# Hybrid RWKV-7 / retention / attention block: a block-diagonal state chain, matmuls issued in groups by tile shape, modulation weights in pairs of blocks

## The chip, the cores and the metric

The kernel runs on one core of a Trainium2 chip. The metric is the device time of one execution in microseconds (us); the kernel before was run three times. A separate execution was profiled, and every row below comes from it.

## The reference

Two layers of one trunk over 512 tokens (256 context tokens, then 256 latent ones) of width 1024. Per layer: a modulated RMSNorm; one input projection; three token mixers side by side (RWKV-7 in both directions, retention, multi-head latent attention); a gated merge; then a modulated RMSNorm and a SwiGLU, dense in layer 0 and top-2 of 8 experts in layer 1. The modulation comes from `c @ w_mod + b_mod`. What matters here is the RWKV-7 mixer, 8 heads of 64 channels, both directions:

```python
def step(S, xs):
    r_t, w_t, k_t, v_t, kk_t, a_t = xs
    sa = jnp.einsum('bhij,bhj->bhi', S, -kk_t)
    S = (S * w_t[:, :, None, :] + sa[..., None] * (kk_t * a_t)[:, :, None, :]
         + v_t[..., None] * k_t[:, :, None, :])
    return S, jnp.einsum('bhij,bhj->bhi', S, r_t)
```

## The kernel before

All data is 32 bit. The projections run with operands split into a high and a low part in the one-pass 32-bit type (`mm3`, L917 to L919, three matmuls); an ordinary 32-bit matmul is issued as two passes, so counts of such matmuls in the trace are twice those of the code.

The RWKV-7 scan is done in chunks of 64 tokens. A *unit* is a pair of heads (`p`, four of them) in one direction (`d`), so a layer has 8 units of 8 chunks. For each unit:

- `rwkv_elem` makes decays and keys; `lora_up` is part of it: a product with the high half `hi` of the weights (L260, 128 rows) and one with the low half `lo` (L261, the 64 rows of the direction).
- `rwkv_prod` makes the products of keys within the chunks (L389, on 64 rows, two halves of the chunks), masks them into `MX`, and calls `rwkv_inverse`, which inverts the unit triangular matrices: much VectorE work, then four groups of 32 x 32 matmuls (L564, L573, L592, L602) into the transposed inverse `TF`, one 64-column block per chunk and head.
- `rwkv_trans` transposes keys and values; the values go to rows 64 to 127 of `UV`.
- `rwkv_chain` goes through the chunks in order. A chunk: L625 (with the state `S`) and L627 (`MX` with `UV`) add up in PSUM; VectorE copies them to `Pb` (L630); L636 multiplies by `TF` per head; ScalarE copies the result into rows 0 to 63 of `UV` (L638); L641 gives the state's update; VectorE adds it (L646). After each four chunks the outputs are made (L658, L662, on 64 columns).

`weave` draws these generators together: while unit u's chain is emitted, products and transposes of u+1, the elements of u+2 and *fill* are emitted between, each in proportion to a written number of steps. Fill is projection work whose results are spilled to DRAM (`spill`) and, in units 0 to 3, the modulation (`mods`). `NFILL` and `MODF` say how many steps of each go into a unit. What fill is left goes under attention and retention (`attend`).

`mods` takes 128-row blocks of `w_mod`; four matmuls of 32 columns each (L1031) per block. It yields after each block; `modnorm`, `ffn`, `run` and `fill` draw these yields. Raw weights of the projections and of the modulation share a ring of four buffers (`wraw`), loaded on SyncE's queue.

The order on each engine isn't that of the program text: a planner places instructions by a rank, which is the place in program order, among those whose operands it reckons to be ready. `tc.high_priority(n)` lowers the rank of what is emitted inside by n.

Of the kernel before, what the change touches and what calls it, by code (L numbers as in the profile page):

```python
# [24 lines left out]
def build_consts():  # L25
# [15 lines left out]

    strict = strict & (p[:, None] >= 64)
# [89 lines left out]
class Kern:  # L132
# [14 lines left out]

    def cst(s, name):
        o, w = CB[name]
        return s.consts[:, o:o + w]  # L150
# [91 lines left out]
    def lora_weights(s, i):  # L242
# [3 lines left out]
        lo = s.tile(s.rp, [128, 512], f"wlo{i}", F32R)  # L246
        for d in range(2):
            own = HRS[d]
            raw = s.tile(s.rp, [128, 512], ("rF", "kF", "vF", "kk")[i * 2 + d])
            for hr in HRS:  # L250
                nc.sync.dma_start(raw[hr], s.I["lw2"][s.l, own, i * 512:i * 512 + 512])
            nc.gpsimd.tensor_copy(hi[:, d], raw)
            nc.gpsimd.tensor_tensor(lo[own], raw[own], hi[own, d].bitcast(F32), ALU.subtract)
        return hi, lo

    def lora_up(s, ps, i, d, p):

        (hi, lo), X = s.lw[i], s.lx[i]
        rows, cols = HRS[d], slice(p * 128, p * 128 + 128)
        s.nc.tensor.matmul(ps, hi[:, d, cols], X[:, d], start=True, stop=False)  # L260
        s.nc.tensor.matmul(ps, lo[rows, cols], X[rows, d], start=False, stop=True)  # L261
# [111 lines left out]
    def rwkv_prod(s, U):  # L373
# [4 lines left out]
        MX = s.mxs[s.nmx % 2]  # L378
        s.nmx += 1
        mk = s.cst(f"mask{U.d}")  # L380
        for half in range(2):
# [4 lines left out]
            for cc in range(4):  # L386
                c = half * 4 + cc
                for h, hr in enumerate(HRS):
                    nc.tensor.matmul(px[h][:, cc * 128:cc * 128 + N], U.BK[hr, c].rearrange("p a b -> p (a b)"), U.LA[hr, c].rearrange("p a b -> p (a b)")[:, 0:N], start=True, stop=True)  # L389
# [12 lines left out]
    def rwkv_trans(s, U):  # L402

        nc, rp = s.nc, s.rp
        ident = s.cst("ident")
        U.BT = BT = s.tile(rp, [128, 8, 128], "BT")
# [13 lines left out]
        for odd in range(2):  # L420
            nc.scalar.copy(UV[64:128].rearrange("p (c o) v -> p c o v", o=2)[:, :, odd], pv[odd * 64:odd * 64 + 64].rearrange("p (c v) -> p c v", v=128))

# [27 lines left out]
    def rwkv_run(s, proj):  # L450

        s.tts = [s.tile(s.rp, [128, 17 * 64], f"TT{j}") for j in range(2)]
        s.las = [s.tile(s.rp, [128, 8, 2, 64], f"LA{j}") for j in range(3)]
        s.mxs = [s.tile(s.rp, [128, 8, 2, 128], f"MX{j}") for j in range(2)]
# [3 lines left out]
        s.ntt = s.nuv = s.nsd = s.nla = s.nmx = 0  # L458
        for t in s.tts + s.sds:
            s.nc.gpsimd.memset(t, 0.0)  # L460
        for t in s.uvs:
            s.nc.gpsimd.memset(t[0:64], 0.0)

        if s.t0:
            for t in s.las:
                s.nc.gpsimd.memset(t[:, 0:s.t0 // 64, 1], 0.0)
            for t in s.mxs:
                s.nc.gpsimd.memset(t[:, 0:s.t0 // 64, :, 64:128], 0.0)
# [14 lines left out]
        for u in range(-1, 8):  # L483
# [21 lines left out]
    def rwkv_inverse(s, Ac, FT):  # L505
# [64 lines left out]
        for u in range(8):  # L570
            for qd in range(4):
                qr = slice(qd * 32, qd * 32 + 32)
                nc.tensor.matmul(pe[qr, u * 32:u * 32 + 32], ET[qr, u, :], Q[qr, u, :], start=True, stop=True)  # L573
# [9 lines left out]
        TT = TF[:, 0:1024].rearrange("p (c h t) -> p c h t", c=8, h=2)  # L583
        for h in range(2):
            a, b = slice(h * 64, h * 64 + 32), slice(h * 64 + 32, h * 64 + 64)
            nc.scalar.mul(TT[0:32, :, h, 0:32], E2T[a], -1.0)
            nc.scalar.mul(TT[32:64, :, h, 32:64], E2T[b], -1.0)
        p2 = s.tile(s.ps, [128, 512], "iv")
        for u in range(8):
            for h in range(2):  # L590
                a, b = slice(h * 64, h * 64 + 32), slice(h * 64 + 32, h * 64 + 64)
                nc.tensor.matmul(p2[b, u * 32:u * 32 + 32], FT[a, u, :], E2[a, u, :], start=True, stop=True)  # L592
# [6 lines left out]
        for u in range(8):  # L599
            for h in range(2):  # L600
                a, b = slice(h * 64, h * 64 + 32), slice(h * 64 + 32, h * 64 + 64)
                nc.tensor.matmul(pg[a, u * 32:u * 32 + 32], Q2[b, u, :], E2T[b, u, :], start=True, stop=True)  # L602
        yield
        for h in range(2):
            a = slice(h * 64, h * 64 + 32)
            nc.scalar.copy(TT[0:32, :, h, 32:64], pg[a, 0:256].rearrange("p (u c) -> p u c", c=32))
        return TF

    def rwkv_chain(s, U):
# [12 lines left out]
        for k, c in enumerate(order):  # L622
            ch = s.tile(s.ps, [128, 512], "ch")
            if k:
                mm(ch[:, 0:128], LA[:, c].rearrange("p a b -> p (a b)"), S[:, k - 1], start=True, stop=False)  # L625
            for h in range(2):
# [8 lines left out]
            for h in range(2):  # L635
                mm(ch[:, 128 + h * 64:192 + h * 64], U.TF[:, (2 * c + h) * 64:(2 * c + h) * 64 + 128], Pb[:, hs[h]], start=True, stop=True)  # L636
# [13 lines left out]
            if c >= c0o and k % 4 == 3:  # L650
# [3 lines left out]
                for j in (g * 4, g * 4 + 2):  # L654
                    cb = j % 4 * 64
                    for odd, hr in enumerate(HRS):
                        if j + odd != order[0]:
                            mm(po[hr, cb:cb + 128], LA[:, j + odd, 1, :], S[:, order.index(j + odd) - 1], start=True, stop=False)  # L658
                    for h in range(2):
                        for odd, hr in enumerate(HRS):  # L660
                            first = j + odd == order[0]
# [1282 lines left out]
```

## Time and profile before

| what | value |
|---|---|
| three runs | 2420.04, 2423.49, 2425.33 us (median 2423.49) |
| the profiled execution's own time | 2412.98 us |
| its span, first to last instruction | 2411.2 us |
| TensorE matmul busy | 2262.6 us (94%) |
| VectorE busy | 1538.5 us (64%) |
| ScalarE busy | 1170.4 us (49%) |
| GpSimd busy | 355.6 us (15%) |
| DMA, mean over the span | 155 GB/s |
| mean granted TensorE clock | 0.97 |

The profiled execution took 1.8 us more than its span, and 10.5 us less than the median of the three runs. Matmuls are pipelined: in a timeline the distance from one start to the next says what one costs, not its duration.

### The profile page before, as it was taken

Reading aid. Unit: us, or ns where it says so; the run is one execution under the profiler, and the core shown is the slowest. Engines: PE = TensorE matmul, PEld = TensorE weight load, DVE = VectorE, ACT = ScalarE, POOL = GpSimd, SP = SyncE. Lnnn points to the kernel's source line nnn. Section 1 sums busy time; section 2 is a strip of 40 time slices with the busy share of each in tenths; the row PEclk is TensorE's granted clock in tenths of the full one; section 3 lists DMA queues with packets and bytes.
Section 4 is the critical chain, followed back from the end, with each engine's and each line's share of the span. In section 5 each row is a group of like instructions: output and inputs, shape, how many; then the busy total and the mean of one; then the engine's idle time right before and its main releaser. Section 6 shows DMA issues by size and latency. Waiting matters only on the chain. (4 is left out here: it accounts for less than half of the span.)

```text
span 2411.2 us, 41643 instructions
## 1 busy us (share of the span) xinstructions
PE 2262.6 (94%) x15772; PEld 1785.6 (74%) x15772; DVE 1538.5 (64%) x2994; ACT 1170.4 (49%) x2150; POOL 355.6 (15%) x307
## 2 busy tenths in 40 slices
PE   7989999999999989999998999999998989999996
PEld 4767777787667767778876777878867768878775
DVE  5776666655566453333227678777567578888897
ACT  4544444544543342222226554565363457777765
POOL 1311112101002210000013221130111211111120
PEclk9999999999999999999999999999899989999998
DMA  7343432223235424443223333322325658988895
GB/s 259 110 141 127 139 122 71 76 87 117 94 113 157 160 81 162 169 162 104 95 79 124 111 113 117 115 65 91 114 71 162 216 174 320 336 306 318 309 319 192
DMA packets 160609, 373.69 MB, mean 155 GB/s; under 512 B 18016, under 2 KB 35424, under 8 KB 160400
## 3 DMA queue, kind: packets, MB, share of 16 engines
q1 hardware_dynamic: 160400, 370.94, 45.9%
q8 instruction: 126, 2.06, 0.4%
q14 instruction: 83, 0.68, 0.1%
HBM read 345.18 MB, written 25.69 MB: 154 GB/s over the span
## 5 line engine op out<-in xcount | busy, mean ns | idle before, releaser
L895 DVE TENSOR_TENSOR wlo<-wraw,whi 128x512 fp32r<-128x512 f32 (+4 forms) x666 | 652.6, 1001 | 347.9 <-ACT whi L893 334.7
L893 ACT CAST whi<-wraw 128x512 fp32r<-128x512 f32 (+4 forms) x666 | 536.8, 820 | 557.2 <-PE mm L918 226.6
L917 PE MATMUL fl<-xh,whi 128*128 128x512 f32 (+1 forms) x816 | 317.0, 389 | 2.8 <-ACT whi L893 2.7
L919 PE MATMUL fl<-xh,wlo 128*128 128x512 f32 (+1 forms) x816 | 306.7, 376 | 6.7 <-DVE wlo L895 6.5
L918 PE MATMUL fl<-xl,whi 128*128 128x512 f32 (+1 forms) x816 | 302.4, 371 | 0.0
L919 PEld LDWEIGHTS fl<-xh,wlo 128*128 128x128 f32 x816 | 157.7, 193 | 31.6 <-DVE wlo L895 10.0
L917 PEld LDWEIGHTS fl<-xh,whi 128*128 128x128 f32 x816 | 158.0, 194 | 27.9 <-issue 6.0
L918 PEld LDWEIGHTS fl<-xl,whi 128*128 128x128 f32 x816 | 158.2, 194 | 21.3 <-issue 4.7
L917 PE MATMUL mm<-xh,whi 128*128 128x512 f32 (+1 forms) x416 | 165.6, 400 | 2.0 <-ACT pad L1797 1.0
L919 PE MATMUL mm<-xh,wlo 128*128 128x512 f32 (+1 forms) x416 | 162.5, 391 | 3.2 <-DVE wlo L895 3.1
L918 PE MATMUL mm<-xl,whi 128*128 128x512 f32 (+1 forms) x416 | 163.5, 393 | 0.0
L918 PE MATMUL mm<-wlo,xgh 128*128 128x512 f32 (+1 forms) x384 | 146.5, 381 | 15.3 <-DVE wlo L895 14.8
L917 PE MATMUL mm<-whi,xgh 128*128 128x512 f32 (+1 forms) x384 | 144.3, 378 | 0.2 <-ACT xs L1665 0.2
L919 PE MATMUL mm<-whi,xgl 128*128 128x512 f32 (+1 forms) x384 | 143.7, 374 | 0.0
L1696 POOL TENSOR_TENSOR H<-H,yt 128x512 f32<-128x512 f32 x29 | 56.1, 1960 | 392.5 <-DVE yt L1695 392.5
L918 PEld LDWEIGHTS mm<-wlo,xgh 128*128 128x128 f32 x384 | 72.2, 188 | 37.0 <-DVE wlo L895 27.0
L917 PEld LDWEIGHTS mm<-xh,whi 128*128 128x128 f32 x416 | 78.3, 189 | 27.3 <-ACT whi L893 4.9
L919 PEld LDWEIGHTS mm<-xh,wlo 128*128 128x128 f32 x416 | 78.4, 188 | 20.9 <-DVE wlo L895 4.9
L636 PEld LDWEIGHTS ch<-Pb,TT 128*128 128x128 f32 x512 | 71.8, 194 | 26.2 <-DVE Pb L630 17.3
L918 PEld LDWEIGHTS mm<-xl,whi 128*128 128x128 f32 x416 | 78.6, 189 | 16.3 <-DVE xl L711 0.8
L646 DVE SCALAR_TENSOR_TENSOR Sd<-ch,e2c,Se 64x64 f32<-64x64 f32 x192 | 53.8, 280 | 56.0 <-PE ch L641 53.4
L636 PE MATMUL ch<-Pb,TT 128*128 128x64 f32 x512 | 79.3, 278 | 8.9 <-DVE Pb L630 8.1
(527 smaller groups left out, 4688.1 us busy)
## 6 DMA issues: line engine op xcount, KB each, us to landing
wraw<-in_ws_dram SPq DMA_DIRECT2D x284, 512.0 KB
wraw<-in_ws_dram SPq DMA_DIRECT2D x302, 256.0 KB
wraw<-in_w_mod_dram SPq DMA_DIRECT2D x96, 256.0 KB
wraw<-in_ws_dram SPq DMA_DIRECT2D x64, 384.0 KB
wraw<-in_w_mod_dram SPq DMA_DIRECT2D x32, 512.0 KB
wm<-in_w_mod_dram SPq DMA_DIRECT2D x32, 256.0 KB
spg<-stg SPq DMA_DIRECT2D x24, 256.0 KB
mth<-spg SPq DMA_DIRECT2D x24, 256.0 KB
```

Source lines behind the costliest of these rows:

```text
L636: mm(ch[:, 128 + h * 64:192 + h * 64], U.TF[:, (2 * c + h) * 64:(2 * c + h) * 64 + 128], Pb[:, hs[h]], start=True, stop=True)
L646: nc.vector.scalar_tensor_tensor(S[hr, k, hr], ch[hr, o], e2c[hr, c, :], Se[hr, hr], ALU.mult, ALU.add)
L893: s.nc.scalar.copy(hi, raw)
L895: s.follow(s.nc.vector.tensor_sub(lo, raw, hi.bitcast(F32)))
L917: mm(out, ah, bh, start=start, stop=False)
L918: mm(out, ah, bl, start=False, stop=False)
L919: mm(out, al, bh, start=False, stop=stop)
L1696: eng.tensor_tensor(s.h[2 + i][:, ns], s.h[2 + i][:, ns], t, ALU.add)
```

## The change

- The chain's product of `MX` with the values is made before the chain, for all eight chunks of a unit at once, in `rwkv_trans`: 16 matmuls on quarter-array tiles (64 rows by 64 columns) into one PSUM tile, copied by ScalarE into rows 0 to 63 of `UV` (the refill). The chain later overwrites those rows as before.
- In a chunk, VectorE adds that part to L625's product, once per head, into the two diagonal blocks of a zeroed `Pd`; for the first chunk it copies. `TF` now holds the two heads' blocks below one another, and one matmul of 128 columns takes the place of the two of 64.
- `lo` of the lora weights has 128 rows with zeros in the other direction's half, so that L261 runs on all 128 rows.
- Groups of matmuls of one tile shape (`rwkv_prod`, the new product, four in `rwkv_inverse`, the outputs, a pair of modulation blocks) are emitted under `together()`, which is `high_priority(60)`.
- `mods` takes two blocks per yield; the step counts that draw it are halved.
- `rwkv_trans` is woven with 28 steps instead of 4; in layer 1, `NFILL` for units is 12 instead of 9.
- `MX` comes from the pool instead of two fixed tiles, and some memsets go.

```diff
+    def together(s):
+        return s.tc.high_priority(60)
...
     def lora_weights
-        lo = s.tile(s.rp, [128, 512], f"wlo{i}", F32R)
+        lo = s.tile(s.rp, [128, 2, 512], f"wlo{i}", F32R)
+        nc.gpsimd.memset(lo.bitcast(F32), 0.0)
...
-            nc.gpsimd.tensor_tensor(lo[own], raw[own], hi[own, d].bitcast(F32), ALU.subtract)
+            nc.gpsimd.tensor_tensor(lo[own, d], raw[own], hi[own, d].bitcast(F32), ALU.subtract)
...
     def lora_up
-        s.nc.tensor.matmul(ps, lo[rows, cols], X[rows, d], start=False, stop=True)
+        s.nc.tensor.matmul(ps, lo[:, d, cols], X[:, d], start=False, stop=True)
...
     def rwkv_trans
+        while U.MX is None:
+            yield
+        pm = s.tile(s.ps, [128, 512], "aa")
+        with s.together():
+            for c in range(8):
+                for h, hr in enumerate(HRS):
+                    nc.tensor.matmul(pm[hr, c * 64:c * 64 + 64], U.MX[64:128, c, h, 0:64], UV[64:128, c, hr], start=True, stop=True)
+        yield
+        for hr in HRS:
+            nc.scalar.copy(UV[0:64, :, hr], pm[hr].rearrange("p (c v) -> p c v", v=64))
...
     def rwkv_run
-        s.tts = [s.tile(s.rp, [128, 17 * 64], f"TT{j}") for j in range(2)]
+        s.tts = [s.tile(s.rp, [128, 9 * 64], f"TT{j}") for j in range(2)]
+        s.pds = [s.tile(s.rp, [128, 128], f"Pd{j}") for j in range(2)]
...
-                st.append((f"trans{u + 1}", s.rwkv_trans(U[u + 1]), 4))
+                st.append((f"trans{u + 1}", s.rwkv_trans(U[u + 1]), 28))
...
     def rwkv_inverse (and so for the other three groups)
-        for u in range(8):
-            for qd in range(4):
-                qr = slice(qd * 32, qd * 32 + 32)
-                nc.tensor.matmul(pq[qr, u * 32:u * 32 + 32], F16[qr, u, :], E[qr, u, :], start=True, stop=True)
+        with s.together():
+            for u in range(8):
+                for qd in range(4):
+                    qr = slice(qd * 32, qd * 32 + 32)
+                    nc.tensor.matmul(pq[qr, u * 32:u * 32 + 32], F16[qr, u, :], E[qr, u, :], start=True, stop=True)
...
     def rwkv_chain
-                mm(ch[:, 0:128], LA[:, c].rearrange("p a b -> p (a b)"), S[:, k - 1], start=True, stop=False)
-            for h in range(2):
-                mm(ch[:, hs[h]], MX[:, c, h], UV[:, c, hs[h]], start=k == 0, stop=k == 0 or h == 1)
-            yield
-            Pb = s.tile(rp, [128, 128], "Pb")
-            nc.vector.tensor_copy(Pb, ch[:, 0:128])
+                mm(ch[:, 0:128], LA[:, c].rearrange("p a b -> p (a b)"), S[:, k - 1], start=True, stop=True)
+                yield
+            Pd = s.pds[k % 2]
+            for hr in hs:
+                if k:
+                    nc.vector.tensor_add(Pd[hr, hr], ch[0:64, hr], UV[0:64, c, hr])
+                else:
+                    nc.vector.tensor_copy(Pd[hr, hr], UV[0:64, c, hr])
...
-            for h in range(2):
-                mm(ch[:, 128 + h * 64:192 + h * 64], U.TF[:, (2 * c + h) * 64:(2 * c + h) * 64 + 128], Pb[:, hs[h]], start=True, stop=True)
+            mm(ch[:, 128:256], U.TF[:, c * 64:c * 64 + 128], Pd, start=True, stop=True)
...
-MODF = [19, 10]
+MODF = [10, 5]
...
-NFILL = [[16, 20] + [13] * 8, [14, 16] + [9] * 8]
+NFILL = [[16, 20] + [13] * 8, [14, 16] + [12] * 8]
...
     def mods
-                for k in range(8):
...
+                for k in range(0, 8, 2):
+                    wm = [s.early.pop((b, q, kk)) if (b, q, kk) in s.early else s.mod_block(l, b, q, kk, s.wp, n) for kk in (k, k + 1)]
+                    with s.together():
+                        for kk, w in zip((k, k + 1), wm):
+                            for j in range(4):
+                                nc.tensor.matmul(ps[j * 32:j * 32 + 32, 0:n * 128].rearrange("p (q x) -> p q x", q=n), s.S[:, kk, :], w[:, :, j], start=kk == 0, stop=kk == 7)
                     yield
...
     def modnorm
-                s.step(mods, 9 if k else 5)
+                s.step(mods, 5 if k else 3)
...
     def ffn
-            s.step(s.gen, 2 if f < 18 else 0)
+            s.step(s.gen, 1 if f < 20 else 0)
```

## Rows read from the trace of the kernel before

**Rows 1.** Stretches: length; busy PE, PEld, DVE, ACT, POOL (instructions); clock, DMA, GB/s.

```profile
150.00:590.00 440.00, 420.76 (x4151) 329.23 (x4149) 282.29 (x685) 198.08 (x445) 72.31 (x62) 0.98 0.35 110
...
1310.00:1740.00 430.00, 406.05 (x4262) 338.97 (x4261) 307.11 (x751) 224.58 (x519) 78.86 (x71) 0.96 0.34 106
...
1985.00:2411.00 426.00, 390.58 (x1839) 319.89 (x1837) 369.14 (x379) 300.25 (x379) 59.98 (x32) 0.98 0.84 300
```

**Rows 2.** Waits of TensorE, 150 to 590 us: total us, times, longest.

```profile
PE ch L625 <- DVE Sd L646: 6.5, 8, 2.9
...
PE fl L919 <- DVE wlo L895: 1.3, 3, 0.8
```

**Rows 3.** Timeline of TensorE, unit 4 of layer 1: start, us, engine, line.

```profile
1583.17 0.39 PE L918 MATMUL fl<-xl,whi 128*128 128x512 f32 x1
1583.40 0.55 PE L636 MATMUL ch<-Pb,TT 128*128 128x64 f32 x4
1583.76 0.48 PE L919 MATMUL fl<-xh,wlo 128*128 128x512 f32 x1
...
1585.66 0.40 PE L260 MATMUL mm<-lx,H 128*128 128x512 f32 x1
1585.99 0.49 PE L261 MATMUL mm<-lx,wlo 64*128 64x512 f32 x1
1586.41 0.49 PE L625 MATMUL ch<-Sd,LA 128*128 128x128 f32 x2
1586.74 0.56 PE L627 MATMUL ch<-SU,MX 128*128 128x64 f32 x4
1587.10 0.47 PE L918 MATMUL fl<-xl,whi 128*128 128x512 f32 x1
...
1595.89 0.38 PE L641 MATMUL ch<-SU,BT 128*128 128x128 f32 x2
1596.02 0.48 PE L918 MATMUL fl<-xl,whi 128*128 128x512 f32 x1
```

**Rows 4.** Timeline of TensorE, groups of small tiles, unit 3 of layer 1.

```profile
1567.11 0.56 PE L592 MATMUL iv<-D,AF 32*32 32x32 f32 x22
1567.60 0.66 PE L636 MATMUL ch<-Pb,TT 128*128 128x64 f32 x4
1568.19 0.37 PE L592 MATMUL iv<-D,AF 32*32 32x32 f32 x10
1568.49 0.39 PE L917 MATMUL fl<-xh,whi 128*128 128x256 f32 x1
...
1569.28 0.45 PE L662 MATMUL oo<-SU,MX 128*64 128x64 f32 x8
1569.56 0.39 PE L658 MATMUL oo<-Sd,LA 128*64 128x128 f32 x4
...
1571.22 0.69 PE L602 MATMUL iv<-F,Q 32*32 32x32 f32 x32
1571.85 0.38 PE L917 MATMUL fl<-xh,whi 128*128 128x256 f32 x1
```

**Rows 5.** Timeline of TensorE, modulation blocks as fill, layer 0.

```profile
318.20 0.64 PE L1031 MATMUL fl<-wraw,S 128*32 128x128 f32 x16
318.77 0.66 PE L636 MATMUL ch<-Pb,TT 128*128 128x64 f32 x4
319.36 0.42 PE L1031 MATMUL fl<-wraw,S 128*32 128x128 f32 x8
319.71 0.50 PE L260 MATMUL mm<-lx,H 128*128 128x512 f32 x1
```

**Rows 6.** Single lines: durations in ns, min/median/max, first and last start.

```profile
L646 DVE SCALAR_TENSOR_TENSOR Sd<-ch,e2c,Se x192: 201/288/294, 155.1 to 1712.2; 64x64 f32<-64x64 f32 x192
...
L421 ACT COPY SU<-aa x32: 577/581/585, 125.5 to 1669.5; 64x512 f32<-64x512 f32 x32
```

**Rows 7.** Waits of SyncE's queue, 150 to 590 us: total us, times, longest.

```profile
SPq L886 <- DVE wlo L895: 115.7, 35, 9.5
```

More of the change, by code (lines that the diff above doesn't have):

```diff
@@ L385, in rwkv_prod @@
             px = [s.tile(s.ps, [128, 512], "aa") for _ in HRS]
[L386 to L389, printed above, removed]
+            with s.together():
+                for cc in range(4):
+                    c = half * 4 + cc
+                    for h, hr in enumerate(HRS):
+                        nc.tensor.matmul(px[h][:, cc * 128:cc * 128 + N], U.BK[hr, c].rearrange("p a b -> p (a b)"), U.LA[hr, c].rearrange("p a b -> p (a b)")[:, 0:N], start=True, stop=True)
             yield
@@ L405, in rwkv_trans @@
         ident = s.cst("ident")
+        U.MX = None
         U.BT = BT = s.tile(rp, [128, 8, 128], "BT")
@@ L569, in rwkv_inverse @@
         pe = s.tile(s.ps, [128, 512], "iv")
[L570 to L573, printed above, removed]
+        with s.together():
+            for u in range(8):
+                for qd in range(4):
+                    qr = slice(qd * 32, qd * 32 + 32)
+                    nc.tensor.matmul(pe[qr, u * 32:u * 32 + 32], ET[qr, u, :], Q[qr, u, :], start=True, stop=True)
         yield
@@ L598, in rwkv_inverse @@
         pg = s.tile(s.ps, [128, 512], "iv")
-        for u in range(8):
-            for h in range(2):
-                a, b = slice(h * 64, h * 64 + 32), slice(h * 64 + 32, h * 64 + 64)
-                nc.tensor.matmul(pg[a, u * 32:u * 32 + 32], Q2[b, u, :], E2T[b, u, :], start=True, stop=True)
+        with s.together():
+            for u in range(8):
+                for h in range(2):
+                    a, b = slice(h * 64, h * 64 + 32), slice(h * 64 + 32, h * 64 + 64)
+                    nc.tensor.matmul(pg[a, u * 32:u * 32 + 32], Q2[b, u, :], E2T[b, u, :], start=True, stop=True)
         yield
@@ L653, in rwkv_chain @@
                 g = c // 4
[L654 to L659, printed above, removed]
-                        for odd, hr in enumerate(HRS):
-                            first = j + odd == order[0]
-                            mm(po[hr, cb + h * 64:cb + h * 64 + 64], MX[:, j + odd, h, 64:128], UV[:, j + odd, hs[h]], start=first, stop=first or h == 1)
+                with s.together():
+                    for j in (g * 4, g * 4 + 2):
+                        cb = j % 4 * 64
+                        for odd, hr in enumerate(HRS):
+                            if j + odd != order[0]:
+                                mm(po[hr, cb:cb + 128], LA[:, j + odd, 1, :], S[:, order.index(j + odd) - 1], start=True, stop=False)
+                        for h in range(2):
+                            for odd, hr in enumerate(HRS):
+                                first = j + odd == order[0]
+                                mm(po[hr, cb + h * 64:cb + h * 64 + 64], MX[:, j + odd, h, 64:128], UV[:, j + odd, hs[h]], start=first, stop=first or h == 1)
                 yield
@@ L1830, in run @@
         s.gen = s.mods(0)
-        s.step(s.gen, 4)
+        s.step(s.gen, 2)
         nc.sync.dma_start(s.consts, s.I["consts"])
```

41 lines of the change are left out of this document (15 added, 26 removed).

## The prediction

> **What bounds the kernel now.** I looked first at the busy time by stretch [rows 1]. In the two stretches in which the recurrence runs (150 to 590 us for layer 0, 1310 to 1740 us for layer 1) the reader is to see TensorE busy for 420.76 of 440 us and 406.05 of 430 us, while VectorE has 282.29 and 307.11 us, ScalarE 198.08 and 224.58 us, and the DMA engines about a third. In the expert stretch (1985 to 2411 us) VectorE with 369.14 of 426 us and the DMA engines at 0.84 stand beside TensorE; no edit touches it. All edits but the modulation pairs act in the first two stretches, so I read those.
>
> Busy time of a pipelined engine can hide slack, so I looked next at who made TensorE wait there: in layer 0's stretch the largest entry is 6.5 us in 8 waits of the chain's first product for the state; waits for projection weights come to 1.3 us [rows 2]. Third, the timeline of TensorE: starts follow each other without holes, a projection matmul of 512 columns every 0.23 us [rows 3], and the chain's short products stand among them. So the order is a good one, the chain's latency is covered by projection work, and in both stretches the time is the sum of what TensorE issues. Work taken from its queue comes off the time until VectorE, which is used to 64% and 71%, gets in the way.
>
> **The change part by part.** There are 2 layers x 8 units x 8 steps = 128 chain steps; 16 units.
>
> (a) *L627 leaves the chain.* The four passes of a step (two products, two passes each) take 0.36 us until the next start, from 1586.74 to 1587.10 us [rows 3]. 128 x 0.36 = 46 us less. The product before it (L625) already stands there, so no return to the projection shape is saved with it.
>
> (b) *Two 64-column products with TT become one of 128 columns.* Today's four passes of 64 columns hold the queue for 0.36 us (1583.40 to 1583.76); the two 128-column passes of L641, the same form as the new one, hold it for 0.13 us (1595.89 to 1596.02) [rows 3]. 0.23 x 128 = 29 us less. That the wider product is the cheaper one says that a pass here costs about the same whatever its columns.
>
> (c) *The L627 work comes back once per unit,* as 16 products, 32 passes of 64 columns on quarter-array tiles. The trace has no 64-row by 64-column tile. Below, the 32-pass group L602 takes 0.63 us with its entry [rows 4], so 16 x 0.63 = 10 us; above, the 0.09 us per pass of L627, 16 x 32 x 0.09 = 46 us, which would give all of (a) back. Nearest are L662's passes, also 64 columns and alternating between two column tiles: 8 in 0.28 us [rows 4], 35 ns each. 32 of them are 1.1 us, and 0.3 us for entry and exit (the price of a break, below) makes 1.4 us: 16 x 1.4 = 23 us more.
>
> (d) *The low half of the lora product on all 128 rows.* Before it TensorE spends 0.33 us on a product that normally takes 0.23, and 0.42 us on L261 itself [rows 3]. 0.33 + 0.42 - 2 x 0.23 = 0.29 us, 32 times: 9 us less. The zero rows cost nothing: a pass has the same columns. A memset of zeros on GpSimd, twice a layer, replaces memsets of similar size; nothing for it.
>
> (e) *Groups kept together.* L592's 32 passes come as 22 and 10 with one chain product between: 0.49 + 0.59 + 0.30 = 1.38 us, of which that product is 0.36 plus 0.09 us of slower restart; the unbroken L602 takes 0.63 us [rows 4]. So a break costs 0.3 us. A unit has eight such groups (four in the inverse, two of L389, two of the output); of the two shown one is broken, so I take four breaks: 16 x 4 x 0.3 = 19 us. Bounds: nothing, if the higher rank does not help, and twice that. Only the matmuls are ranked higher, so they cannot start before their operands; what they delay is at most one group, about 0.6 us, of products whose wait is covered.
>
> (f) *Modulation blocks in pairs.* A single block of 8 passes holds the queue 0.35 us, a run of 16 passes 0.57 us [rows 5], so a pair saves 2 x 0.35 - 0.57 = 0.13 us. By the loop counts 96 blocks are fed into the chain stretches: 48 x 0.13 = 6 us less. The blocks of the start and of the feed-forward are already issued two or more at a time: nothing there.
>
> (g) *VectorE and ScalarE.* One copy of 128 columns becomes two additions of 64 x 64, so each step has one operation more. Nearest is L646, 64 x 64 with one operand in PSUM: 201 ns at least, 288 in the median [rows 6]. 128 x 0.288 = 37 us more, 18 per layer (13 by the least); the first steps, from SBUF, will be cheaper. ScalarE gets 32 copies of the L421 form, 0.581 us [rows 6]: 19 us more. Both lie under TensorE's work: VectorE goes to (282 + 18) of about (440 - 43) us, 76%, and in layer 1 to (307 + 18) of (430 - 43), 84%. The chain's latency falls by (a) and (b), 0.59 us a step, and rises by one addition, 0.29 us.
>
> (h) *Fill counts.* Three more quanta per unit of layer 1 and the halved step counts move projection work and its loads from the attention stretch into the chain stretch. The same matmuls run; I take nothing, since it costs cover in one place and gives it in the other.
>
> Sum: -46 - 29 + 23 - 9 - 19 - 6 = -86 us. What is late next is VectorE's answer to the chain, so I let a tenth, 8 us, come back as waits: -78 us. From the profiled execution's 2412.98 us this gives 2335 us; that execution ran 10.5 us under the median of 2423.49 us, so beside the median it is **2345 us**.
>
> **The rivals.**
>
> *VectorE takes over.* After (b) each step waits for two additions, queued behind inverse operations of up to 1 us. If VectorE can't be packed beyond 76% in these stretches, layer 0 still loses its 43 us (300 / 0.76 = 395 us), but layer 1 can't fall below 325 / 0.76 = 428 us: about 45 us in all, **2378 us**. For it: 71% today in layer 1. Against it: 87% in the expert stretch [rows 1].
>
> *Passes cost what their columns cost.* Then 0.36 us for L627 and L636 would be mostly a wait that stays, and the 0.13 us of two 128-column passes says that four of 64 need 0.13 as well: (a) gives 17 us, (b) nothing, the sum is -17 + 23 - 9 - 19 - 6 = -28 us, **2395 us**. [...] The 0.36 and 0.13 us stand against it here, and I give it 7 in 100.
>
> *Groups don't hold together.* The rank alone does not keep an earlier-ranked product out that becomes ready in mid-group. Then (e) is 0 and (f) stays: -67 us, less a tenth, **2363 us**. It lies within the likeliest case's range.
>
> *Slower: pairs starve the ring of raw weights.* A pair holds two of four buffers until its second block has landed. The queue of loads already waits for buffers: 115.7 us in 35 waits for the low half, 3.3 us each [rows 7]. If every one of 48 pairs passes one such wait on to TensorE, it is 48 x 3.3 = 158 us, less 78: 80 us slower, **2504 us**. It decides from 1.6 us a pair on. Against it: TensorE's waits for weights in that stretch come to 1.3 us [rows 2], so the ring runs ahead. 6 in 100.
>
> *No difference:* (c) at its upper bound and VectorE in the way together give back nearly all. 6 in 100.
>
> **How the numbers follow.** The forecast, TensorE's queue with most of the sum kept, including the unheld groups, gets 0.59; VectorE taking over 0.22; passes by columns 0.07; no difference 0.06; slower 0.06. The likeliest case's own range is 2305 to 2370 us: its lower end is the sum with (c) at 10 and (e) at 38 us, -118 us, its upper end the unheld groups with a little more given back. For 8 in 10 the range must take in VectorE's case and most of the columns' case: **2302 to 2398 us**. A measurement of this kernel can tell about 0.2%, 5 us. Faster by more than that: 0.59 + 0.22 + 0.07 = 0.88; within it 0.06; slower 0.06.
>
> **What would show it.** In the changed profile the chain's step has one product before the additions and one of 128 x 128 after, two passes each; the quarter-array group of 32 passes takes about 1.4 us; the lora's second product follows its first by 0.23 us; the inverse's groups stand as runs of 64 and 32. TensorE's busy share in both stretches stays above 92% and VectorE's rises to about 76 and 84%; the stretches are some 40 us shorter each. The prediction is wrong if TensorE shows waits for the additions of 20 us or more in a layer, if the new group takes 2.5 us, or if TensorE waits for raw weights.

## The result, and the profile after

The change makes the kernel slower: 2602.56 us median (2585.05 to 2607.9, 4 runs) against 2421.76 us (2412.31 to 2425.33, 4 runs), a ratio of 1.0722 with a 95% interval of 1.0675 to 1.0769. The profiled execution took 2600.33 us, its span is 2598.5 us, its mean granted clock 0.944 (before: 0.97). That is 181 us more, where 78 us less was forecast.

The lines of the code move: L625 is L639 after, L636 is L651, L641 is L656, the additions are L644, L646 is L661, L389 is L392, L1031 is L1046, L917 to L919 are L933 to L935, and L627's work is L432, in `rwkv_trans`.

First question: where the time went. The stages below are distances on TensorE's timeline between starts of products (a chain stage: from the first to the last product with `BT`, L641 before; "down to chain": from the last product of the feed-forward to the first with `BT`). All other stages agree within 5 us. e1 to e15 are experiments, described below.

| stage, us | before | after | e1 | e3 | e13 | e5 | e6 |
|---|---|---|---|---|---|---|---|
| start to chain, layer 0 | 148 | 182 | 150 | 173 | 163 | 150 | 151 |
| chain, layer 0 | 398 | 434 | 384 | 433 | 395 | 383 | 395 |
| gate and up, layer 0 | 281 | 333 | 281 | 280 | 284 | 281 | 283 |
| down to chain, layer 1 | 117 | 135 | 118 | 127 | 125 | 117 | 117 |
| chain, layer 1 | 325 | 374 | 347 | 372 | 346 | 320 | 375 |
| attention, layer 1 | 185 | 184 | 183 | 183 | 185 | 189 | 185 |

The loss isn't in the chains alone: gate and up, where of all edits only the modulation pairs act, lose 52 us, the start 34 us. The busy time by stretch (columns as in [rows 1]; before: the chains of layer 0 and 1; after: chain of layer 0, gate and up, chain of layer 1, experts) says that in these stretches TensorE is still busy nearly all the time, and that in the chains VectorE is not:

```profile
148.00:547.00 399.00, 380.93 (x3949) 297.74 (x3950) 256.04 (x615) 179.32 (x410) 63.70 (x50) 0.97 0.34 108
1387.00:1712.00 325.00, 311.13 (x3579) 261.74 (x3578) 240.04 (x604) 173.05 (x413) 56.51 (x49) 0.98 0.32 100
...
182.00:616.00 434.00, 409.95 (x3751) 281.40 (x3751) 263.10 (x675) 184.70 (x422) 66.64 (x50) 0.94 0.30 96
947.00:1270.00 323.00, 320.36 (x1353) 217.31 (x1352) 91.57 (x114) 79.58 (x105) 0.00 (x0) 0.97 0.36 125
1528.00:1901.00 373.00, 353.54 (x3604) 278.84 (x3602) 261.35 (x683) 192.60 (x455) 56.19 (x49) 0.92 0.31 100
2146.00:2598.00 452.00, 417.20 (x1964) 342.02 (x1962) 391.24 (x400) 321.22 (x404) 59.99 (x32) 0.98 0.83 297
```

VectorE has 263 of 434 and 261 of 373 us in the chains, 61% and 70%: not the rival. TensorE's waits in layer 0's chain: for the state they fell (6.5 us in [rows 2]), the product behind the additions waits 8.5 us for them (before, 1.2 us for the copy L630 in their place), raw weights nearly none:

```profile
PE ch L651 <- DVE Pd L644: 8.5, 9, 1.9
...
PE fl L1046 <- DMA wraw<-in_w_mod_dram: 1.8, 3, 1.0
PE ch L639 <- DVE Sd L661: 1.7, 5, 0.6
```

So most of the time is TensorE being busy for longer: 2408.8 us in all against 2262.6, 146 us more, while its idle time over the whole span grew by 41 us. The groups of the page say with what (tile, partitions x columns, count | busy us, mean ns; first before, then after):

```profile
L1031 PE MATMUL fl<-wraw,S 128*32 128x128 f32 x768 | 41.2, 287 | 4.1 <-ACT stg L960 2.6 <-DMA wraw<-in_w_mod_dram 1.3
L389 PE MATMUL aa<-LA,BK 64*128 64x128 f32 x384 | 36.2, 295 | 0.0
L1031 PE MATMUL aa<-wraw,S 128*32 128x256 f32 x256 | 18.8, 386 | 0.0
...
L1046 PE MATMUL fl<-wraw,S 128*32 128x128 f32 x768 | 75.4, 302 | 1.8 <-DMA wraw<-in_w_mod_dram 1.8
...
L392 PE MATMUL aa<-LA,BK 64*128 64x128 f32 x384 | 63.2, 308 | 5.5 <-POOL BK L368 5.1 <-ACT BT L419 0.3
...
L1046 PE MATMUL aa<-wraw,S 128*32 128x256 f32 x256 | 56.5, 403 | 2.0 <-DMA wraw<-in_w_mod_dram 2.0
```

The counts and shapes are the same, the mean of one is 4 to 5% longer, and the busy time of the group is 1.7 to 3 times as long: its members overlap one another less, more of them stand alone. The timeline shows it, first in gate and up, one modulation pair (start, us):

```profile
1106.80 0.63 PE L1046 MATMUL aa<-wraw,S 128*32 128x256 f32 x6
1107.36 0.49 PE L933 MATMUL mm<-xh,whi 128*128 128x512 f32 x1
1107.78 0.62 PE L1046 MATMUL aa<-wraw,S 128*32 128x256 f32 x2
1108.33 0.49 PE L934 MATMUL mm<-xl,whi 128*128 128x512 f32 x1
1108.76 0.62 PE L1046 MATMUL aa<-wraw,S 128*32 128x256 f32 x2
...
1111.68 0.62 PE L1046 MATMUL aa<-wraw,S 128*32 128x256 f32 x2
1112.23 0.50 PE L935 MATMUL mm<-xh,wlo 128*128 128x512 f32 x1
```

A zipper: after the first three matmuls (6 passes) one modulation matmul and one projection matmul take turns. The pair runs from 1106.80 to 1112.23, 5.43 us, and five projection matmuls of 0.23 us stand in it, so it costs 5.43 - 1.15 = 4.3 us. Before, a pair stands whole here:

```profile
946.33 1.07 PE L1031 MATMUL aa<-wraw,S 128*32 128x256 f32 x16
947.33 0.50 PE L917 MATMUL mm<-xh,whi 128*128 128x512 f32 x1
```

1.00 us. The difference is 3.3 us. Of the stage's 16 pairs (256 passes by 16) 12 are cut into the same six parts, which makes 40 us; one is cut into eight and one into five, and two stand whole. So these cuts are most of the 52 us that the stage lost. In the chains modulation blocks are cut by other neighbours:

```profile
254.51 0.44 PE L417 MATMUL aa<-consts,BK 128*128 128x128 f32 x2
254.88 0.41 PE L1046 MATMUL fl<-wraw,S 128*32 128x128 f32 x2
255.22 0.33 PE L417 MATMUL aa<-consts,BK 128*128 128x128 f32 x1
```

Two passes of a modulation block hold the queue for 0.34 us here; 16 in a row held it for 0.57 [rows 5]. Counted over the timeline, the modulation's matmuls stand in 116 unbroken runs before and in 267 after, 171 of these with 2 passes; L389's in 56 and 113; of the inverse's four groups the first two in 33 and 37 before and 31 and 29 after, the last two in 25 and 18 before and 51 and 41 after (16 would be whole). The edit that was to keep groups together takes most of them apart.

Why it can do so: inside `high_priority(60)` the rank is set back by 60, and on leaving it returns to the value that it had, so a group takes no ranks of its own. Its i-th matmul has rank n - 60 + i, and up to 60 instructions emitted just before have the ranks n - 60 to n - 1. Wherever those are still waiting for their turn, there is one of them and one of the group at each rank, and a planner that goes by rank issues them in turn. The planner's own choices are not in a trace; e4 and e13 below test this by changing nothing but ranks.

The clock has a part in it too. The granted clock of TensorE has two levels in these traces: each of the 38 records of it before and of the 72 after is 1 or 0.5. By the mean clocks, 0.97 and 0.944, TensorE spent some 145 us of the span at the lower level before and 291 us after; without the rank (e1, 0.959) it is 198 us. At 0.5 one 512-column projection matmul of the kernel before starts 0.43 us after another (878.87 to 879.30 us), at 1 0.23 us [rows 3], so nearly half of the time at 0.5 is lost there. If half of all time at 0.5 is lost, that is an estimated 46 us of the 174 us that the rank costs (e1 below), which leaves some 128 us for the rest, the cuts above all. That the cuts bring the clock down is not shown separately.

### The profile page after: what moved, and what is told of

Its sections match the earlier page's. It is cut to its first block, busy times and chain, and to the rows that moved or that the text cites. A ratio compares the mean times of both kernels' runs of the same rounds, so it can differ in the third digit from the quotient of the medians.

```text
span 2598.5 us, 41145 instructions
## 1 busy us (share of the span) xinstructions
PE 2408.8 (93%) x15516; PEld 1788.4 (69%) x15516; DVE 1556.7 (60%) x3122; ACT 1186.0 (46%) x2182; POOL 355.1 (14%) x309
## 5 line engine op out<-in xcount | busy, mean ns | idle before, releaser
L911 DVE TENSOR_TENSOR wlo<-wraw,whi 128x512 fp32r<-128x512 f32 (+4 forms) x666 | 642.9, 985 | 377.4 <-ACT whi L909 359.5
L933 PE MATMUL fl<-xh,whi 128*128 128x512 f32 (+1 forms) x816 | 328.1, 402 | 0.0
L935 PE MATMUL fl<-xh,wlo 128*128 128x512 f32 (+1 forms) x816 | 319.9, 392 | 1.6 <-DVE wlo L911 1.6
L934 PE MATMUL fl<-xl,whi 128*128 128x512 f32 (+1 forms) x816 | 319.1, 391 | 0.0
L935 PEld LDWEIGHTS fl<-xh,wlo 128*128 128x128 f32 x816 | 162.1, 199 | 31.4 <-issue 9.3
L933 PEld LDWEIGHTS fl<-xh,whi 128*128 128x128 f32 x816 | 162.0, 199 | 27.4 <-issue 10.5
L935 PE MATMUL mm<-xh,wlo 128*128 128x512 f32 (+1 forms) x416 | 167.4, 402 | 3.1 <-DVE wlo L911 3.1
L933 PE MATMUL mm<-xh,whi 128*128 128x512 f32 (+1 forms) x416 | 168.8, 407 | 0.7 <-ACT gt L1087 0.7
L933 PE MATMUL mm<-whi,xgh 128*128 128x512 f32 (+1 forms) x384 | 144.2, 378 | 0.2 <-ACT xs L1680 0.2
L935 PE MATMUL mm<-whi,xgl 128*128 128x512 f32 (+1 forms) x384 | 143.6, 374 | 0.0
L935 PEld LDWEIGHTS mm<-xh,wlo 128*128 128x128 f32 x416 | 79.6, 191 | 31.9 <-issue 8.6
L933 PEld LDWEIGHTS mm<-xh,whi 128*128 128x128 f32 x416 | 79.3, 191 | 30.5 <-issue 12.5
L392 PE MATMUL aa<-LA,BK 64*128 64x128 f32 (+1 forms) x512 | 86.1, 317 | 7.2 <-POOL BK L368 5.8
L392 PEld LDWEIGHTS aa<-LA,BK 64*128 64x128 f32 x512 | 64.6, 204 | 28.1 <-issue 11.4
L933 PEld LDWEIGHTS mm<-whi,xgh 128*128 128x128 f32 x384 | 72.2, 188 | 11.2 <-ACT xs L1680 0.4
```

Of the source, the lines that this page charges most:

```text
L911: s.follow(s.nc.vector.tensor_sub(lo, raw, hi.bitcast(F32)))
L933: mm(out, ah, bh, start=start, stop=False)
L934: mm(out, ah, bl, start=False, stop=False)
L935: mm(out, al, bh, start=False, stop=stop)
```

## The experiments

Two theories at first. A: the rank scatters the groups, and each change of tile shape costs. B: VectorE's second addition, or the weights' ring, slows the chain, and the scatter is beside the point.

**e1: no rank.** The changed kernel with `together()` doing nothing.

```diff
-        return s.tc.high_priority(60)
+        return ExitStack()
```

> The changed kernel with no group ranked ahead: the planner sees the matmuls at their place in program order, all else stays. Theory 1, the rank scatters the groups (modulation passes stand in twos between projection matmuls, products of two groups alternate) and costs all that was lost and more: about 2350 to 2380 us, with modulation runs of 16 passes. Rival A, the new chain (two additions, the refill, the wait of the transposes for the masked products) is what costs: 2550 us or more. Rival B, pairs of modulation blocks starve the ring of raw weights: also 2550 us or more, with waits of TensorE for raw weights.

Measured: 2428.86 us (10 runs), ratio 1.0036 (1.001 to 1.0063). The rank costs 2602.56 - 2428.86 = 174 us. But the kernel is still not faster than before: 2350 to 2380 us was expected if scatter were all.

**e2: rank alone.** The kernel before with its own groups under `high_priority(60)`, nothing else.

> The kernel before with only its own groups (products, inverse, outputs, each modulation block) ranked 60 ahead; chain, lora, counts as before. Theory 1: 2560 to 2620 us, with modulation passes in twos and about 250 runs of that shape instead of 116. Rivals A and B: within 1% of the kernel before, about 2420 us.

Measured: 2626.0 us, 1.0843 (1.0789 to 1.0897). The rank makes the old kernel as slow, and slower, without refill, pairs or a second addition. B falls as the main cause. The modulation stands in 185 runs here, not the 250 expected, and L389's groups in 118; layer 0's chain takes 483 us. The mean clock is 0.924, about 400 us at the lower level: by the same estimate as above, half of the 255 us more than before, some 128 of the 204 us that this kernel loses go with the clock.

**e3: modulation pairs not ranked.** The changed kernel, the pair's `with s.together()` replaced by `with ExitStack()`.

> The changed kernel with the modulation pairs alone not ranked ahead. Theory 1: the stages where modulation runs beside projections (start, feed-forward, before layer 1's chain) fall back to before's lengths, some 52 us in the feed-forward and 20 to 50 us elsewhere; 2490 to 2530 us. Rival A: about 2600 us. Rival B: about 2600 us, since pairs stay pairs.

Measured: 2535.29 us, 1.049 (1.0438 to 1.0542). Of the 174 us, 67 belong to the modulation, 53 of them in gate and up, which are back at 280 us. Layer 0's chain stays at 433 us: what it lost doesn't hang on the modulation, but on the other groups, which are still ranked (L389's stand in 112 runs).

**e4: ranks of their own.** The changed kernel, each group ranked far ahead of everything, at 40 ranks that no other has.

```diff
-        return s.tc.high_priority(60)
+        s.ngroup += 1
+        return s.tc.high_priority(s.tc.cur_priority + 100000 - 40 * s.ngroup)
```

> The changed kernel with each group's ranks far ahead of all ordinary work and apart from every other group's, so that no pending product has a rank inside a group. Theory 1: groups stay whole (runs of 64 and 32 passes in the inverse, 16 or more for modulation) and the time is that of the kernel without ranks or some 10 to 20 us less: 2335 to 2370 us. If ranking ahead is harmful by what it delays, and not by scattering, it stays near 2600 us.

Measured: 2461.38 us, 1.0158 (1.0109 to 1.0208). The inverse's four groups stand whole (16 runs each for 16 units), the modulation in 125 runs. 141 of the 174 us are back with the groups further ahead than before, but not the 2335 to 2370 us expected. A part of what being ahead costs is waiting for loads, since a modulation matmul now stands before work that is ready; these waits are 9.9 us, against 1.0 us in e1:

```profile
PE aa L1048 <- DMA wraw<-in_w_mod_dram: 5.4, 14, 1.9
PE fl L1048 <- DMA wraw<-in_w_mod_dram: 4.5, 8, 1.5
```

TensorE's busy time is also 36 us longer than in e1 (2248.6 against 2213.0 us); what makes it so is open.

**e13: one rank per group.** Still 60 ahead, but each matmul is ranked by itself, so that a whole group has the one rank n - 60.

```diff
+    def gmm(s, *a, **k):
+        with s.tc.high_priority(60):
+            s.nc.tensor.matmul(*a, **k)
...
-                    nc.tensor.matmul(pm[hr, c * 64:c * 64 + 64], ...)
+                    s.gmm(pm[hr, c * 64:c * 64 + 64], ...)
```

> The changed kernel with one edit: every matmul of a group is ranked 60 ahead by itself, so that all matmuls of a group have one and the same rank, 60 before the place where the group is emitted, in place of a run of 16 to 32 ranks that overlaps those of other products. Theory A (the ranks that overlap scatter the groups, and the scatter costs): the groups are whole again, the modulation matmuls stand in some 120 runs instead of 266, and the time falls by 130 us or more, to 2430 to 2470 us. Theory B (issuing the groups ahead of other work costs, whole or not): 2560 to 2610 us, the stage of the feed-forward of layer 0 still some 50 us longer than before.

Measured: 2456.88 us, 1.0147 (1.0117 to 1.0176): 146 us come back, at the same 60 ranks ahead. The modulation's groups are whole again, in 119 runs, by the groups of its page (L152 is the helper):

```profile
L152 PE MATMUL fl<-wraw,S 128*32 128x128 f32 x768 | 40.6, 281 | 2.3 <-DMA wraw<-in_w_mod_dram 1.8 <-ACT stg L980 0.2
...
L152 PE MATMUL aa<-wraw,S 128*32 128x256 f32 x256 | 18.6, 398 | 2.3 <-DMA wraw<-in_w_mod_dram 2.3
```

40.6 and 18.6 us, as before (41.2 and 18.8). L389's matmuls stand in 60 runs and are busy for 50.7 us, between the 36.2 before and the 63.2 after. A is shown: ranks that overlap others' ranks cost 146 us, being early some 28 us more.

**e8: whole groups without the fill's move.** e5 (below) with e4's ranks for the chain's groups alone.

> The fifth experiment's kernel with groups whole by ranks of their own, modulation pairs left out of it. If broken groups were worth the 19 us of term (e): 10 to 19 us below that kernel, about 2375 us. If ranking ahead delays the chain's own products as much as it saves in breaks: the same or slower, 2390 to 2410 us.

Measured: 2434.4 us, 1.0053 (1.0023 to 1.0084), 32 us more than e5 without any rank, and more than either theory expected. Whole groups issued ahead of other work are no gain either.

**e5, e6, e12: the fill counts.** e5 is e1 with `NFILL` of layer 1 back at 9, e12 the same at 6; e6 is the kernel before with 12.

```diff
-NFILL = [[16, 20] + [13] * 8, [14, 16] + [12] * 8]
+NFILL = [[16, 20] + [13] * 8, [14, 16] + [9] * 8]
```

> The changed kernel without ranks and with layer 1's fill back at 9 quanta a unit. Theory 2, the 24 quanta of projection work moved into layer 1's chain cost their full 40 us there and give nothing back in attention, which other things bound: 2385 to 2395 us, layer 1's chain about 308 us long instead of 347, attention still about 183 us. Rival C, VectorE's answers set the chain's pace, so that less fill only turns into waits: 2420 to 2430 us, with the chain still about 340 us.

> The kernel before with layer 1's fill at 12 quanta a unit and nothing else changed. Theory 2: layer 1's chain about 35 us longer, attention unchanged; about 2455 us. As predicted (what moves costs in one place and gives in the other): within 5 us of the kernel before.

> The kernel without rank and with fill 9, with the fill count of layer 1 lowered once more, to 6. Theory A (in chain stage 1 each fill step that was moved in costs TensorE time there, and attention 1 has room for it, as the step from 12 to 9 gave 27 to 55 us): about 2385 to 2395 us, chain stage 1 shorter by 10 to 25 us and attention 1 longer by less. Theory B (at 9 the chain is bound by its own dependent steps and not by fill, and attention 1 is full): 2400 to 2425 us, attention 1 longer by as much as chain stage 1 gets shorter or by more.

Measured: e5 2401.93 us, 0.9906 (0.9873 to 0.994), faster than both kernels; e6 2472.43 us, 1.0208 (1.0149 to 1.0268); e12 2419.09 us, 0.999 (0.9966 to 1.0014). Moving three quanta per unit into layer 1's chain costs 27 us from e5 to e1 (31 us by the ratios) and some 50 us from before to e6. In e6 the chain gets 50 us longer and the attention, from which the work was taken, no shorter (attention before; then chain and attention of e6):

```profile
1712.00:1896.00 184.00, 165.91 (x1032) 134.12 (x1030) 123.57 (x316) 83.49 (x180) 34.33 (x44) 0.92 0.44 135
...
1390.00:1765.00 375.00, 353.76 (x3806) 302.82 (x3806) 254.06 (x622) 186.97 (x442) 54.61 (x49) 0.92 0.32 103
1765.00:1950.00 185.00, 144.78 (x802) 110.25 (x800) 110.52 (x297) 70.47 (x151) 35.37 (x44) 0.85 0.33 102
```

TensorE is busy 144.78 of 185 us there, at a clock of 0.85: 21 us less than before, and the stage is as long. In the chain the clock is 0.92, 0.98 before. Taking more out of the chain (e12) doesn't shorten it either (321 us against 320), and the attention grows from 189 to 203 us. The two chains of layer 1, e5 and then e12:

```profile
1373.00:1693.00 320.00, 292.22 (x3457) 235.79 (x3455) 252.56 (x667) 181.90 (x432) 52.97 (x49) 0.97 0.33 104
...
1379.00:1700.00 321.00, 280.64 (x3193) 216.01 (x3192) 241.55 (x645) 166.79 (x399) 52.58 (x49) 0.90 0.26 83
```

TensorE is busy 12 us less and has fewer matmuls, but the clock is 0.90 in place of 0.97 and its waits come to 39 us in place of 27. Of the three counts tried, 9 is the best.

**e7, e9, e10, e11: parts of the chain's edits, unranked, with layer 1's fill at 9.** e9 and e10 are built on the kernel before, e7 and e11 are the changed kernel with the other named edits undone. e7: refill and block-diagonal product, without lora and pairs. e9: pairs alone. e10: pairs, lora and the block-diagonal product without refill (the two blocks copied by VectorE and ScalarE). e11: pairs and refill, with one 64x128 addition and the two TT products as before.

```diff
e10
-            Pb = s.tile(rp, [128, 128], "Pb")
-            nc.vector.tensor_copy(Pb, ch[:, 0:128])
+            Pd = s.pds[k % 2]
+            nc.vector.tensor_copy(Pd[0:64, 0:64], ch[0:64, 0:64])
+            nc.scalar.copy(Pd[64:128, 64:128], ch[0:64, 64:128])
...
e11
+                nc.vector.tensor_add(Pd[0:64], ch[0:64, 0:128], UV[0:64, c])
...
```

> The kernel before with the block-diagonal chain and the refill alone; lora, modulation, ranks and fill counts as before. By the prediction's terms (a) to (c) -52 us of TensorE's queue; from the first experiment's waits some 30 us of it come back: 2395 to 2405 us. Rival C: no gain at all, about 2420 us.

> The kernel before with one part of the change alone: modulation weights two blocks at a time, not ranked ahead, the step counts of the modulation streams halved. Theory A (the pairs are the small term (f) of the prediction, 6 us, and the 30 us between the kernel with whole own-ranked groups and the kernel without any rank come from elsewhere): about 2415 us, chain stage 0 at 395 to 400 us. Theory B (the pairs, by halving the changes of tile shape in the fill work of both chains, are what makes the kernel with fill 9 faster than before): about 2395 to 2402 us, with chain stage 0 at 383 to 388 us as there. Theory C (pairs starve the ring of raw weights): above 2430 us, with longer DMA waits of the modulation matmuls.

> The kernel before with lora on 128 rows, modulation pairs unranked, and the merged block-diagonal TT product, but without refill: the MX.UV product stays inside the chain as before and the diagonal blocks of P are copied in parallel by VectorE and ScalarE. Theory A (TensorE time saved in the chain comes back to the total when VectorE gets no further operation): about 2421 minus 29 minus 9 minus 6, some 2380 to 2390 us. Theory B (TensorE time saved in the chains is given back as waits and half-clock time, whatever VectorE does): 2405 to 2425 us. In the trace A wants the waits of the chain's products for VectorE at the level of before (some 18 us in chain stage 0 and 14 in stage 1), B wants them up by most of what the products lost.

> The kernel without rank and with fill 9, but without the merged block-diagonal product and with lora on 64 rows as before: refill outside the chain, one VectorE addition of 64x128, two TT products. Theory A (VectorE's second addition is what gives the saved TensorE time back): its waits for the addition and for the state stay near those of before, and by (a), (c) and (f) the time is 2421 minus 23 minus 6, about 2390 to 2395 us. Theory B (any shortening of TensorE's share of a chain step lengthens the wait for the state, which VectorE sets): 2400 to 2425 us with the waits for the state up by 10 us or more per stage.

Measured: e7 2431.96 us, 1.0033 (1.0003 to 1.0062); e9 2411.29 us, 0.9969 (0.9947 to 0.9992); e10 2403.46 us, 0.992 (0.989 to 0.9949); e11 2421.35 us, 1.0 (0.9979 to 1.0021). Pairs are worth 7.5 us by the ratio (2 to 13 by its interval). The refill, 23 us by (a) and (c), is worth nothing or less, and not because of a second addition (e11 has none), nor because of waits: TensorE's waits in e11's chains are 34 us, 30 before. e7 lies above what either of its theories gave.

**e14, e15: the passes put back.** e14 is the kernel before with L627 issued twice, the second time into columns that nobody reads. e15 is e11 with two 64-column products that nobody reads where L627 stood.

```diff
e14
                 mm(ch[:, hs[h]], MX[:, c, h], UV[:, c, hs[h]], start=k == 0, stop=k == 0 or h == 1)
+            for h in range(2):
+                mm(ch[:, 384 + h * 64:448 + h * 64], MX[:, c, h], UV[:, c, hs[h]], start=True, stop=True)
```

> The kernel before with the product of MX and UV issued once more in every chain step, into columns of PSUM that nobody reads: 4 more passes of 64 columns in each of 128 steps, with the same operands, so ready when the first is. Theory A (in the chain stretches the time is the sum of what TensorE issues, each such four passes 0.36 us, as term (a) of the prediction has it): 46 us more, 2468 us. Theory A', the same with the passes cheap behind others of their shape (0.11 to 0.13 us a step as the trace has them for four passes without a wait): 14 to 17 us more, about 2437 us. Theory B (the chain's own dependence sets the stretches, TensorE has room): within 5 us of before.

> The kernel with refill and one addition, with two products of 64 columns that nobody reads put into each chain step where the product of MX and UV stood before (the operands are the block of LA and UV, the shapes are the same). Theory A (the refill takes 46 us from TensorE's queue, and something else in the refill gives it back): 2421 plus 40 to 46, about 2465 us. Theory A' (the four passes are worth only what they cost without a wait): 2421 plus 14 to 17, about 2437 us. Theory B (the time does not follow these passes, because TensorE waits in their place or its clock falls): 2416 to 2426 us, and the half-clock time of the chain stretches lower than in the kernel without the products.

Measured: e14 2467.21 us, 1.02 (1.0168 to 1.0233), 45.5 us more; (a) says 46. e15 2436.94 us, 1.0068 (1.0042 to 1.0094), 15.6 us more than e11. The same passes cost 46 us in one kernel and 16 in the other. 2437 us is what Theory A' gave, but its reason doesn't hold: in e15 the four passes take 0.37 us to the next start in the median, 56 us over the two chains, and in the kernel before no four such passes take under 0.36 us. What differs is the clock. The chains of e11, then of e15:

```profile
149.00:546.00 397.00, 381.43 (x3908) 281.12 (x3908) 251.84 (x613) 184.30 (x421) 65.67 (x50) 0.92 0.34 107
1389.00:1719.00 330.00, 310.87 (x3573) 253.55 (x3572) 239.30 (x605) 181.03 (x430) 55.88 (x49) 0.94 0.32 100
```

```profile
148.00:549.00 401.00, 386.48 (x4158) 299.10 (x4157) 251.06 (x613) 184.10 (x421) 66.92 (x50) 0.97 0.33 106
1393.00:1724.00 331.00, 312.33 (x3796) 262.61 (x3794) 239.68 (x602) 179.47 (x427) 53.02 (x49) 1.00 0.31 98
```

With the useless passes the clock is 0.97 and 1.00, without them 0.92 and 0.94, and the stages are only 4 and 1 us longer (of the 14 us between the two profiled executions, 9 lie behind the second chain). It isn't one execution alone: over all runs the mean clock was 0.952 to 0.959 in e11 and 0.956 to 0.971 in e15. e11 pays for the passes it saved with time at the lower level, 0.5 (102 us in its two chains, by the clock records of its trace). One such fall in e11, first two windows, then the timeline:

```profile
262.00:280.00 18.00, 17.99 (x210) 13.78 (x212) 6.87 (x22) 9.26 (x23) 2.55 (x3) 1.00 0.31 105
280.00:307.00 27.00, 26.73 (x184) 16.37 (x185) 15.12 (x52) 8.15 (x18) 3.30 (x4) 0.51 0.39 127
```

```profile
270.30 0.40 PE L934 MATMUL fl<-xh,wlo 128*128 128x512 f32 x1
270.63 0.71 PE L391 MATMUL aa<-LA,BK 64*128 64x128 f32 x6
271.27 0.65 PE L1045 MATMUL fl<-wraw,S 128*32 128x128 f32 x16
271.84 0.66 PE L650 MATMUL ch<-Pd,TT 128*128 128x64 f32 x4
272.43 0.62 PE L1045 MATMUL fl<-wraw,S 128*32 128x128 f32 x10
...
289.35 1.12 PE L650 MATMUL ch<-Pd,TT 128*128 128x64 f32 x4
290.39 0.66 PE L1045 MATMUL fl<-wraw,S 128*32 128x128 f32 x8
```

From 270.63 on no 512-column product is issued, only short ones, and at 280 us the clock falls, to 0.51 in the mean of the next 27 us; TensorE was busy 17.99 of the 18 us before. The four passes of L650 then hold the queue for 1.04 us, against 0.59.

With that the chain's books can be drawn up, as an estimate. With two levels, 1 and 0.5, the time at the lower one is 2 x (1 - mean clock) x span (of the whole execution); half of it is taken as lost, as above and as if TensorE set the time throughout. Waits are those of TensorE in the two chain stretches, all rows of the waits view added. "Saved" takes (a) and (c) as forecast, 46 and 23, pairs as in e9, and for the TT and lora products the start-to-start distances added over e10's chains and before's: 25 and 5 us less.

| us, against before | saved | waits | lower clock / 2 | sum | medians |
|---|---|---|---|---|---|
| e14 | +46 | 25 - 30 | (143 - 145) / 2 | +40 | +46 |
| e11 | -46 + 23 - 7.5 | 34 - 30 | (223 - 145) / 2 | +12 | 0 |
| e15 | +23 - 7.5 | 31 - 30 | (161 - 145) / 2 | +24 | +15 |
| e10 | -25 - 5 - 7.5 | 46 - 30 | (144 - 145) / 2 | -22 | -18 |
| e7 | -46 + 23 - 25 | 46 - 30 | (214 - 145) / 2 | +2 | +8 |
| e5 | -46 + 23 - 25 - 5 - 7.5 | 56 - 30 | (172 - 145) / 2 | -21 | -23 |

The sums meet the medians within 12 us, with both signs; a term of 10 us can't be told from that. In e11 and e7 the clock takes the refill's gain; where the chain's links get shorter (e10, e5), TensorE waits more.

## Why the prediction was wrong, point by point

**The step that failed is (e).** It said that groups ranked higher stay together, and took "nothing, if the higher rank does not help" as the lower bound. I had a price for a break, 0.3 us, and never asked whether the edit could make breaks. It makes over 200 in the two groups counted above: the term was -19 us and measured +174 (e1). The price itself was half of what it is in gate and up, where five breaks cost 3.3 us, 0.66 us each; the count was the larger error. An estimated 46 of the 174 us are lower clock, which the prediction, in which the time is the sum of what TensorE issues, has no term for. The rival that groups don't hold together stopped at zero for the same reason. The sign that was named for it, runs of 64 and 32 in the inverse, failed in the changed kernel (51 and 41 runs in its last two groups, for 16). The description of the planner, that a rank is the place in program order, was enough to see that n - 60 is a place that others have.

**(h) was not nothing.** It cost 27 us (e5 to e1). The argument that what it costs in one place it gives in the other failed on the side of attention: the work taken out there left its length as it was (185 us in e6), at a lower clock.

**The tenth given back was too little.** Without rank and fill, (a) to (d) and (f) sum to -67 us, and e5 measured -23. Some 26 us came back as waits for VectorE and ScalarE, 14 us as lower clock, and (b) and (d) were 25 and 5 us, not 29 and 9. VectorE's share was 61% and 70% after and 69% and 79% in e5 (266.02 of 383 us and 252.56 of 320 us), so it can be packed beyond the 76% that its rival took as the most. Whether the waits come from the length of its answers or from operations queued before them was not measured.

**What held.** (a) at 0.36 us a step: e14 measured 45.5 us for 46, so for added passes the time did follow TensorE's queue; for removed ones (e11) it didn't. (f): 7.5 us for 6. (c): where the 32 passes stand whole, as here in e5, they take 1.08 us to the next start, against 1.4 us forecast with entry and exit. Seven of e5's 16 groups stand whole; all 16 together take 22 us, against 23 forecast:

```profile
390.52 1.15 PE L432 MATMUL aa<-SU,MX 64*64 64x64 f32 x32
391.60 0.49 PE L639 MATMUL ch<-Sd,LA 128*128 128x128 f32 x2
```

(g) an addition takes 217 ns, less than the 288 ns of [rows 6], a first step's copy from SBUF 186 ns, and TensorE's waits for it, 8.5 us in layer 0's chain, stay under the 20 us a layer that was named as the sign of an error (duration ns, min/median/max):

```profile
L644 DVE TENSOR_TENSOR Pd<-ch,SU x224: 206/217/220, 184.3 to 1903.7; 64x64 f32<-64x64 f32 x112
```

(b) and (d) as mechanisms, in e10 (L642 is the merged product, L265 and L266 the lora products):

```profile
1560.69 0.45 PE L642 MATMUL ch<-Pd,TT 128*128 128x128 f32 x2
1560.89 0.48 PE L925 MATMUL fl<-xh,wlo 128*128 128x512 f32 x1
...
1564.61 0.49 PE L265 MATMUL mm<-lx,H 128*128 128x512 f32 x1
1564.94 0.39 PE L266 MATMUL mm<-lx,wlo 128*128 128x512 f32 x1
1565.17 0.38 PE L423 MATMUL aa<-consts,vR 128*128 128x128 f32 x2
```

The merged product holds the queue for 0.20 us where four 64-column passes held it for 0.36 [rows 3], and L266 for 0.23 where it was 0.42. The 0.13 us of L641 was too short a model for the new product (0.24 us in the median), but the four passes it replaces take 0.47 in the median, so the saving nearly came out, in part by luck. The rival "passes cost what their columns cost" fell with it: the same 256 columns took 0.20 us in two passes and 0.36 us in four.

**The other rivals.** VectorE taking over and the starved ring didn't happen: TensorE's waits for raw modulation weights in layer 0's chain are 1.8 us after. That the time went the way of the "slower" rival is chance: its cause, the ring, is not what the runs show. "No difference" is near what e1 gives, for reasons that it didn't name.

## What to carry to other kernels

A priority that is set back for a group and then restored gives the group ranks that others hold; count the unbroken runs of a tile shape in the timeline before believing that it groups anything, and give a group one rank, or none (none was the better here, by 28 us). A price for a break is a price for every break that the edit can make, so its lower bound isn't zero. Time saved on a busy TensorE was time here only where the clock held (0.92 and 0.94 in e11's chains, and no gain) and the next link of the chain was ready (56 us of waits in e5, 30 before): look at granted clock and waits of the stretch before counting passes as gained.

## What the runs showed of the hardware that was not expected

TensorE's granted clock fell to a mean of 0.51 over 27 us while the engine was issuing nearly without a hole: it was busy for 17.99 of the 18 us before the fall in e11 and for 26.73 of the 27 us after it (the ends of matmuls are modelled in the profile, but their starts in the rows above follow each other without a gap). The trace shows it in a stretch of short products. Not every fall comes at a busy engine: of the nine in e11's two chains, three come after 10 us in which TensorE was busy for 98% or more, the other six after 70 to 91%; of the 17 in the two chains after, five and twelve (66 to 96%).

Work that nobody reads raised the mean clock of the two chains from 0.92 and 0.94 to 0.97 and 1.00 (e15), at stages 4 and 1 us longer. What makes the clock fall, and why removing L627 makes for more time at the lower level (in the two chains 31 us before and 102 us in e11, by the trace's clock records), stays open.
